# Attention layer of a two-layer encoder: key norms in a projection bank, key rounding ordered behind the exponential

## Chip, cores and metric

One core of a Trainium2 chip runs one program. The metric is the device time of one execution in microseconds (us), median over runs.

## What is computed

Two sequences of 512 tokens, each with 16 meta tokens in front (T = 528), go through two layers. Layer one is a gated DeltaNet and is not touched. Layer two is an attention over 16 heads whose queries and keys are normalised by their root mean square. Cut to what matters here:

```python
kv = (ckv @ w_ukv).reshape(B, L, 16, 128 + 128)
k = concat([kv[..., :128], broadcast(k_pe)])      # 192 wide
k = k * rsqrt(mean(k * k) + eps) * gain           # per token and head
s = einsum(q, k) * scale
o = softmax(s) @ v
y = (o * silu(z)) @ w_out
```

## The kernel before, in words

Every matmul operand is split into a rounded high half and a remainder (names ending in H and L, or wh and wl for weights), and three matmuls replace one (`mm3`, lines 74 to 76). ScalarE (ACT) rounds, VectorE (DVE) or GpSimd (POOL) subtracts (the helper at line 87). Weights come in on SyncE's queue (SP) as `wraw` (L210), ACT rounds them to `wh` (L213), POOL makes `wl`.

Layer two works in 16 units of two heads, eight per sequence. `run` writes the order of the program by hand: for step n = 0 to 7 of a unit (two heads times four query blocks) it issues a piece of the next unit's head, then the scores of the next step, then the output of this step. The head's pieces are: n=0 `pair_k` (key projection, four halves, each in a bank tagged `pj`, and the norms of the keys), n=1 `pair_qrope`, n=2 `pair_z` of this unit's second head, n=3 `pair_q` of the first head, n=4 `pair_v`, n=5 `pair_q` of the second head and `pair_knorm` twice, n=6 `pair_z` of the next unit's first head. A scheduler then orders each engine's instructions; within one engine they run in that order, and a waiting instruction holds up those behind it.

PSUM has eight banks: `pj` two, `S` (scores) two of two banks each, `tr` one, `x` one. In `x` lie, in program order per unit, the sums of squares of the keys (L966, n=0), the output products of steps 1 and 3 (L1099 is their last matmul), the sums of squares of the queries (L995, n=5) and the output products of steps 5 and 7.

The way of the key norms: `pair_k` copies the projected keys to `kr` (L959, ACT; one buffer), squares them (L961, L962, ACT), adds them up in `sqH` (L963, POOL), sums over the partitions with 12 small matmuls (L966, PE), adds the shared term (L967, DVE), takes the power -1/2 (L91, POOL, `rk`), writes to memory (L971) and reads it back broadcast to all partitions as `rs` (L973), both on SP. `pair_knorm` multiplies: `kr` by `rs` (L1030, DVE), rounded to `kH` (L378, ACT) with remainder `kL` (L87, DVE); and the shared rotary part by `rs` into `acc` (L1033, POOL), rounded to `kst` (L1035, ACT), remainder by DVE. `pair_knorm` is traced inside `issue_after` blocks, which put each of its instructions on an engine behind a given instruction of that same engine: on POOL behind the last `wl`, on DVE behind the last row maximum `mx` (L1064). On ACT it has no such order.

One step of attention: scores on PE (L74 to L76, L1060, L1061), `mx` (L1064, L1065, DVE), exponential to `P` (L1068, ACT), its scaling (L1069, L1071, DVE), transposes (L1083 for the meta tokens, into the used score bank, L1085 into `tr`), rounding and remainders (`pst` L1088, L1089; `hnH` L1091), output product in `x`, and L1100 (DVE), which reads `x`. The gate of `pair_z` is a tanh on ACT (L1046) and a product on DVE (L1047), which frees the `pj` bank.

Of the kernel before, what the change touches and what calls it, by code (L numbers as in the profile page):

```python
# [11 lines left out]
AF = mybir.ActivationFunctionType  # L12
# [11 lines left out]
class Trunk:  # L24
    def __init__(self, ctx, tc, ins, outs):
        self.tc, self.nc, self.ins, self.outs = tc, tc.nc, ins, outs
        self.ctx = ctx
        self.cn = ctx.enter_context(tc.tile_pool(name="cn", bufs=1))
        self.dr = ctx.enter_context(tc.tile_pool(name="dr", space=DRAM, bufs=1))
        self.sa = ctx.enter_context(tc.tile_pool(name="sa", bufs=1, reuse_waits="tile"))  # L30
        self.n = 0
        self.inner = None
        self.last_mx = None
        self.next_pool(self.BUFS1, self.PBUFS1)

    def next_pool(self, bufs, pbufs):
# [909 lines left out]
    def pair_k(self, u):  # L946
        nc = self.nc
        V, A, G, PE = nc.vector, nc.scalar, nc.gpsimd, nc.tensor
        UKV, c, hs = self.ins["mla_w_ukv"][0], u["c"], u["hs"]
        ckv = c["ckv"]  # L950
        kr = u["kr"] = self.t("kr", [128, 2, T])
        rk = self.t("rk", [88, 2, 6])
        kk = self.t("sqH", [128, T])
        sq = self.t("raw", [128, T])
        for j, h in enumerate(hs):
            w = self.weights([(0, UKV[:, 256 * h:256 * h + 128])], 2, hk=2)
            for c0 in KC:
                ps = self.project(w, ckv, 2, c0, 264)
                A.copy(kr[:, j, c0:c0 + 264], ps)  # L959
            o, nn = self.SIDES[j]  # L960
            A.activation(kk[o], kr[nn, j], AF.Square)  # L961
            A.activation(sq[o], kr[o, j], AF.Square)  # L962
            G.tensor_tensor(kk[o], kk[o], sq[o], op=ALU.add)  # L963
        ps = self.p("x", [88, 6, 2])
        for i in range(6):
            PE.matmul(ps[:, i], kk[:, 88 * i:88 * i + 88], self.two, start=True, stop=True)  # L966
        V.scalar_tensor_tensor(rk, ps.rearrange("p i j -> p j i"), 1.0 / 192, c["kss"].unsqueeze(1).to_broadcast([88, 2, 6]), op0=ALU.mult, op1=ALU.add)  # L967
        rf = rk.rearrange("p j i -> p (j i)")
        self.rsqrt(rf, rf)
        rkd = self.d("rkd", [2, T])  # L970
        nc.sync.dma_start(rkd.rearrange("j (i p) -> p j i", p=88), rk)  # L971
        rs = u["rs"] = self.t("rs2", [128, 2, T])
        nc.sync.dma_start(rs, rkd.rearrange("j t -> (j t)").unsqueeze(0).to_broadcast([128, 2 * T]).rearrange("p (j t) -> p j t", j=2))  # L973
# [75 lines left out]
    def pair_scores(self, u, j, qt):  # L1049
        nc = self.nc  # L1050
        V, A, G, PE = nc.vector, nc.scalar, nc.gpsimd, nc.tensor
        (qH, qL), (kH, kL) = u["q"][j], u["k"][j]
        SQ, RL, kst, qs = u["SQ"], u["RL"], u["kst"][j], u["qs"]
        cs = slice(128 * qt, 128 * qt + 128)
        S = self.p("S", [128, 2, 512])
        for ci, c0 in enumerate(KC):
            kc = slice(c0, c0 + 264)
            so = S[:, ci, 0:264]
            self.mm3(so, (qH[:, cs], qL[:, cs]), (kH[:, kc], kL[:, kc]), last=False)
            PE.matmul(so, SQ[j][:, cs], kst[:, kc], start=False, stop=False)  # L1060
            PE.matmul(so, RL[j][:, cs], kst[:, kc], start=False, stop=True)  # L1061
        Sv = S[:, :, 0:264]
        mx = self.t("mx", [128, 1])
        self.last_mx = V.tensor_reduce(mx, Sv, axis=AX.XY, op=ALU.max, negate=True)  # L1064
        V.tensor_scalar(mx, mx, qs[j][:, qt:qt + 1], None, op0=ALU.mult)  # L1065
        P = self.t("P", [128, 2, 264])
        sm = self.t("sm", [128, 1])
        A.activation(P, Sv, AF.Exp, bias=mx, scale=qs[j][:, qt:qt + 1], accum_out=sm)  # L1068
        V.reciprocal(sm, sm)  # L1069
        P = P.rearrange("p a b -> p (a b)")  # L1070
        V.tensor_scalar(P, P, sm, None, op0=ALU.mult)  # L1071
        u["SP"] = S, P
# [31 lines left out]
    def run(self, rc, rs):  # L1104
# [76 lines left out]
        def head(u):  # L1181
            self.pair_k(u)
            yield
            self.pair_qrope(u)
            yield
            if u["hp"]:
                yield
            self.pair_q(u, 0)
            yield
            if u["hp"]:  # L1190
                self.pair_v(u)
                yield
            self.pair_q(u, 1)
            with ExitStack() as behind:
                for x in [self.last_wl] + ([self.last_mx] if self.last_mx is not None else []):
                    behind.enter_context(self.tc.issue_after(x.ins))
                self.pair_knorm(u, 0)
                self.pair_knorm(u, 1)
            yield
            self.pair_z(u, 0)  # L1200
            yield
            if u["hp"] == 0:
                self.pair_v(u)
                yield
# [13 lines left out]

        ends = [self.out_proj(y2[s], I["mla_w_out"][0], h1[s], hq[s], NM, 512, [tC, tA], finish(s)) for s in range(2)]
        fill = chain(self.l2_prep(0, h1[0], rsd[0], ctx[0]), head(units[0]))  # L1220
        S = self.p("S", [128, 2, 512])
        pss[1] += [S[:, c, 0:264] for c in range(2)]
# [10 lines left out]
        for i, u in enumerate(units):  # L1233
            edge = i % 8 == 7
            if not edge:
                fill = head(units[i + 1])
            else:
                fill = chain(self.l2_prep(1, h1[1], rsd[1], ctx[1]), head(units[8])) if i == 7 else ends[0]
            zat = 0 if i == 15 else 2
            for n in range(8):  # L1240
                if n == zat and i != 7:
                    self.pair_z(u, 1)
                for _ in range((2, 1, 2, 2, 2, 2, 2, 2)[n] if i == 7 else int(n > 0 or not edge)):
                    next(fill, None)
                if i == 6 and n == 7:
                    self.pair_z(units[7], 1)
                S, P = u["SP"]
                if n < 7:
                    self.pair_scores(u, (n + 1) // 4, (n + 1) % 4)
                elif i == 7:  # L1250
                    drain(fill)
                    self.pair_scores(units[8], 0, 0)
                elif i < 15:
                    self.pair_scores(units[i + 1], 0, 0)
                self.pair_out(u, n // 4, n % 4, S, P)
# [48 lines left out]
```

## Time and profile before

| | us |
|---|---|
| median of three runs (lowest, highest) | 2698.04 (2696.45, 2699.07) |
| the profiled execution | 2700.19 |
| its span, first to last instruction | 2698.5 |
| PE busy | 2500.3 (93%) |
| DVE busy | 1755.9 (65%) |
| ACT busy | 1452.6 (54%) |
| POOL busy | 1270.0 (47%) |
| mean granted clock of PE | 0.957 |

Layer two's attention runs from about 1560 to 2480 us of the span. [...] Busy time of PE is modelled and counts a matmul at half clock in full length, so idle time and half clock have to be read separately.

### The profile page before, as it was taken

Reading aid. Unit: us, or ns where it says so; the run is one execution under the profiler, and the core shown is the slowest. Engines: PE = TensorE matmul, PEld = TensorE weight load, DVE = VectorE, ACT = ScalarE, POOL = GpSimd, SP = SyncE. Lnnn points to the kernel's source line nnn. Section 1 sums busy time; section 2 is a strip of 40 time slices with the busy share of each in tenths; the row PEclk is TensorE's granted clock in tenths of the full one; section 3 lists DMA queues with packets and bytes.
Section 4 is the critical chain, followed back from the end, with each engine's and each line's share of the span. In section 5 each row is a group of like instructions: output and inputs, shape, how many; then the busy total and the mean of one; then the engine's idle time right before and its main releaser. Section 6 shows DMA issues by size and latency. Waiting matters only on the chain. (4 is left out here: it accounts for less than half of the span.)

```text
span 2698.5 us, 51896 instructions
## 1 busy us (share of the span) xinstructions
PE 2500.3 (93%) x19083; PEld 2237.2 (83%) x19083; DVE 1755.9 (65%) x3915; ACT 1452.6 (54%) x3522; POOL 1270.0 (47%) x1255
## 2 busy tenths in 40 slices
PE   8899999999999999899999999998998989999999
PEld 7888888878888888788989888887887878887787
DVE  6888887777897777886554356555665656566421
ACT  5445555556555555645545466555556555655432
POOL 5544554435445444533445555444436454544243
PEclk9999999989999999989999899999999999999999
DMA  3222222221222243225475423232322322225475
GB/s 101 67 51 59 56 62 57 70 61 48 62 63 59 53 125 83 78 70 152 121 229 160 125 73 80 67 66 73 91 79 76 79 67 71 66 66 152 136 231 148
DMA packets 448511, 245.14 MB, mean 91 GB/s; under 512 B 131132, under 2 KB 408878, under 8 KB 448256
## 3 DMA queue, kind: packets, MB, share of 16 engines
q1 hardware_dynamic: 448256, 241.82, 33.6%
q8 instruction: 150, 2.46, 0.4%
q14 instruction: 105, 0.86, 0.1%
HBM read 190.72 MB, written 42.08 MB: 86 GB/s over the span
## 5 line engine op out<-in xcount | busy, mean ns | idle before, releaser
L87 POOL TENSOR_TENSOR wl<-wraw,wh 128x512 fp32r<-128x512 f32 (+2 forms) x512 | 661.5, 1294 | 805.4 <-ACT wh L213 744.4
L74 PE MATMUL pj<-hnH,wh 128*128 128x264 f32 (+4 forms) x2080 | 634.1, 306 | 20.0 <-DVE zs L624 10.6
L76 PE MATMUL pj<-hnH,wl 128*128 128x264 f32 (+3 forms) x2080 | 633.6, 306 | 0.5 <-POOL wl L87 0.5
L75 PE MATMUL pj<-hnL,wh 128*128 128x264 f32 (+3 forms) x2080 | 628.9, 303 | 4.5 <-DVE hnL L774 4.5
L213 ACT CAST wh<-wraw 128x512 fp32r<-128x512 f32 (+2 forms) x512 | 306.9, 602 | 312.7 <-PE pj L75 203.2
L74 PEld LDWEIGHTS pj<-hnH,wh 128*128 128x128 f32 (+1 forms) x2080 | 402.5, 194 | 37.6 <-DVE zs L624 12.5
L75 PEld LDWEIGHTS pj<-hnL,wh 128*128 128x128 f32 (+1 forms) x2080 | 402.7, 194 | 18.6 <-DVE hnL L774 5.1
L76 PEld LDWEIGHTS pj<-hnH,wl 128*128 128x128 f32 (+1 forms) x2080 | 401.9, 193 | 15.5 <-issue 3.7
L74 PE MATMUL pj<-h2H,wh 128*128 128x512 f32 (+1 forms) x544 | 207.0, 383 | 5.0 <-ACT h2H L769 3.0
L76 PE MATMUL pj<-h2H,wl 128*128 128x512 f32 (+1 forms) x544 | 207.3, 382 | 0.0
L75 PE MATMUL pj<-h2L,wh 128*128 128x512 f32 (+1 forms) x544 | 206.2, 380 | 0.7 <-DVE h2L L87 0.7
L1064 DVE TENSOR_REDUCE mx<-S 128x1 f32<-128x528 f32 x128 | 89.7, 702 | 77.1 <-PE S L1061 76.7
L74 PEld LDWEIGHTS pj<-h2H,wh 128*128 128x128 f32 x544 | 103.1, 191 | 24.7 <-ACT h2H L769 3.5
L364 DVE SCALAR_TENSOR_TENSOR acc<-raw,vec,acc 128x528 f32<-128x528 f32 x128 | 117.5, 921 | 4.4 <-ACT acc L362 3.3
L75 PEld LDWEIGHTS pj<-h2L,wh 128*128 128x128 f32 x544 | 103.2, 190 | 18.9 <-DVE h2L L87 2.1
L76 PEld LDWEIGHTS pj<-h2H,wl 128*128 128x128 f32 x544 | 103.4, 190 | 17.9 <-POOL wl L87 0.2
L1068 ACT ACTIVATE P<-S,mx,qs 128x528 f32<-128x528 f32 x128 | 101.2, 790 | 31.0 <-DVE mx L1065 29.9
L364 DVE SCALAR_TENSOR_TENSOR kq<-raw,vec,kq 128x528 f32<-128x528 f32 x128 | 110.6, 864 | 9.4 <-ACT kq L362 8.4
L783 DVE TENSOR_TENSOR raw<-raw,pj 128x512 f32<-128x512 f32 (+1 forms) x54 | 31.2, 580 | 125.1 <-PE pj L76 117.8
L722 POOL TENSOR_TENSOR oa<-oa,ot 128x256 f32<-128x256 f32 (+1 forms) x80 | 68.2, 853 | 81.1 <-DVE ot L720 80.9
L87 DVE TENSOR_TENSOR hnH<-tr,hnH 128x512 fp32r<-128x512 f32 x128 | 87.8, 686 | 27.6 <-ACT hnH L1091 26.0
L494 DVE TENSOR_TENSOR Yt<-Bl,Y 66x15 f32<-66x15 f32 (+7 forms) x240 | 85.5, 356 | 23.4 <-POOL Bl L486 18.9
(483 smaller groups left out, 6848.2 us busy)
## 6 DMA issues: line engine op xcount, KB each, us to landing
wraw<-in_gdn_w_in_dram SPq DMA_DIRECT2D x192, 256.0 KB
wraw<-in_mla_w_in_dram SPq DMA_DIRECT2D x88, 256.0 KB
wraw<-in_gdn_w_out_dram SPq DMA_DIRECT2D x64, 256.0 KB
wraw<-in_mla_w_out_dram SPq DMA_DIRECT2D x64, 256.0 KB
acc<-y SPq DMA_DIRECT2D x32, 264.0 KB
rs<-rkd SPq DMA_DIRECT2D x16, 528.0 KB
y<-y SPq DMA_DIRECT2D x64, 128.0 KB
wraw<-in_mla_w_ukv_dram SPq DMA_DIRECT2D x64, 128.0 KB
```

The source lines that it names most:

```text
L74: mm(out, ah, bh, start=first, stop=False)
L75: mm(out, ah, bl, start=False, stop=False)
L76: mm(out, al, bh, start=False, stop=last)
L87: return eng.tensor_tensor(out, a, hi, op=ALU.subtract)
L213: nc.scalar.copy(wh, raw)
L364: nc.vector.scalar_tensor_tensor(acc, raw[:, j:j + T], self.convw(j, u), acc, op0=ALU.mult, op1=ALU.add)
L494: V.tensor_tensor(tv, Bl[:, r + 1:16, r:r + 1].to_broadcast([66, m, c]), Y[:, r:r + 1, 0:c].to_broadcast([66, m, c]), op=ALU.mult)
L722: G.tensor_tensor(oa[:n, i], oa[:n, i], t, op=ALU.add)
L783: nc.vector.tensor_tensor(r[:, c0:c0 + chunk], r[:, c0:c0 + chunk], ps, op=ALU.add)
L1064: self.last_mx = V.tensor_reduce(mx, Sv, axis=AX.XY, op=ALU.max, negate=True)
L1068: A.activation(P, Sv, AF.Exp, bias=mx, scale=qs[j][:, qt:qt + 1], accum_out=sm)
```

## The change

The sums of squares of the keys get a bank tagged `pj` instead of `x`. The last exponential is remembered, and `pair_knorm`'s ACT instructions (both `kH` and both `kst`) are put behind it. At that point of the program the last maximum and the last exponential are those of step 5, the second query block of the unit's second head. (The program traces `pair_knorm` at n=5, when the scores of step 5 have been traced.) Nothing is computed differently.

```diff
-        self.last_mx = None
+        self.last_mx = self.last_P = None
...
             G.tensor_tensor(kk[o], kk[o], sq[o], op=ALU.add)
-        ps = self.p("x", [88, 6, 2])
+        ps = self.p("pj", [88, 6, 2])
         for i in range(6):
             PE.matmul(ps[:, i], kk[:, 88 * i:88 * i + 88], self.two, start=True, stop=True)
...
-        A.activation(P, Sv, AF.Exp, bias=mx, scale=qs[j][:, qt:qt + 1], accum_out=sm)
+        self.last_P = A.activation(P, Sv, AF.Exp, bias=mx, scale=qs[j][:, qt:qt + 1], accum_out=sm)
...
             with ExitStack() as behind:
-                for x in [self.last_wl] + ([self.last_mx] if self.last_mx is not None else []):
+                for x in [self.last_wl] + ([self.last_mx, self.last_P] if self.last_mx is not None else []):
                     behind.enter_context(self.tc.issue_after(x.ins))
                 self.pair_knorm(u, 0)
                 self.pair_knorm(u, 1)
```

## Rows read from the trace of the kernel before

**Rows 1.** Page, part 1: busy time, share of the span, instructions.
```profile
PE 2500.3 (93%) x19083; PEld 2237.2 (83%) x19083; DVE 1755.9 (65%) x3915; ACT 1452.6 (54%) x3522; POOL 1270.0 (47%) x1255
```

**Rows 2.** PE's waits, 1560 to 2480 us: total, times, longest.
```profile
PE pj L74 <- DVE zs L1047: 34.9, 8, 5.7
PE pj L74 <- DVE hnL L87: 16.5, 3, 7.4
...
PE pj L74 <- ACT kr L959: 8.5, 17, 1.0
```

**Rows 3.** One unit: stretch, length, busy PE, PEld, DVE, ACT, POOL, PEclk, DMA share, GB/s.
```profile
2204.74:2263.63 58.89, 51.96 (x332) 46.60 (x331) 34.83 (x73) 33.38 (x76) 26.48 (x20) 0.94 0.27 68
```

**Rows 4.** PE in order of time, parts of that unit: start, length, [idle before, releaser].
```profile
2204.74 1.03 PE L966 MATMUL x<-two,sqH 128*88 128x2 f32 x12
...
2218.84 0.40 PE L76 MATMUL pj<-h2H,wl 128*128 128x512 f32 x1
...
2220.16 0.36 PE L76 MATMUL pj<-ckvH,wl 128*128 128x264 f32 x1
2225.87 0.59 PE L74 MATMUL pj<-ckvH,wh 128*128 128x264 f32 x1 [5.35 <-DVE zs L1047]
...
2229.33 0.42 PE L1061 MATMUL S<-kst,RL 128*128 128x264 f32 x1
...
2235.76 0.39 PE L74 MATMUL pj<-ckvH,wh 128*128 128x264 f32 x1 [0.55 <-ACT kr L959]
...
2237.20 0.28 PE L76 MATMUL pj<-ckvH,wl 128*128 128x264 f32 x1
...
2238.41 0.50 PE L74 MATMUL pj<-cqH,wh 128*128 128x512 f32 x1 [0.38 <-ACT kr L959]
```

**Rows 5.** DVE in order of time, the same unit.
```profile
2225.12 0.69 DVE L1047 SCALAR_TENSOR_TENSOR zs<-zs,pj 128x512 f32<-128x512 f32 x1 [5.36 <-ACT zs L1046]
...
2232.92 0.21 DVE L1065 TENSOR_SCALAR mx<-mx,qs 128x1 f32<-128x1 f32 x1
```

**Rows 6.** ACT in order of time, the same unit.
```profile
2223.45 0.63 ACT L1035 CAST kst<-acc 128x528 fp32r<-128x528 f32 x1 [7.13 <-POOL acc L1033]
...
2224.50 0.59 ACT L1046 ACTIVATE zs<-pj 128x512 f32<-128x512 f32 x1
...
2233.84 0.79 ACT L1068 ACTIVATE P<-S,mx,qs 128x528 f32<-128x528 f32 x1
...
2235.33 0.66 ACT L959 COPY kr<-pj 128x264 f32<-128x264 f32 x2 [0.61 <-DVE kL L87]
...
2238.78 0.38 ACT L959 COPY kr<-pj 128x264 f32<-128x264 f32 x1
```

**Rows 7.** POOL in order of time, the same unit.
```profile
2207.65 2.27 POOL L91 TENSOR_TENSOR rk<-rk,mhalf 88x12 f32<-88x12 f32 x1
...
2222.11 2.55 POOL L1033 TENSOR_TENSOR acc<-kpr,rs 128x528 f32<-128x528 f32 x2 [6.79 <-DMA rs<-rkd]
...
2241.64 1.34 POOL L963 TENSOR_TENSOR sqH<-sqH,raw 64x528 f32<-64x528 f32 x1 [1.15 <-PE S L1083]
```

**Rows 8.** SP's queue in order of time, the same unit.
```profile
2209.94 0.32 SPq L971 DMA_DIRECT2D rkd<-rk  x1
...
2217.06 0.34 SPq L973 DMA_DIRECT2D rs<-rkd  x1
```

**Rows 9.** Waits of POOL and ACT, 1560 to 2480 us: total, times, longest.
```profile
POOL acc L1033 <- DMA rs<-rkd: 91.2, 14, 9.7
...
ACT kst L1035 <- POOL acc L1033: 92.1, 14, 7.5
```

**Rows 10.** Stretches after an idle time of PE, columns as in rows 3.
```profile
2226.00:2228.00 2.00, 2.00 (x9) 2.00 (x10) 1.38 (x4) 1.46 (x4) 0.00 (x0) 0.50 0.35 100
...
2174.00:2180.00 6.00, 5.04 (x21) 4.69 (x21) 2.91 (x8) 5.03 (x13) 4.28 (x3) 0.50 0.00 0
```

**Rows 11.** PE in order of time, another unit.
```profile
2172.47 0.39 PE L74 MATMUL S<-kH,qH 128*128 128x264 f32 x1 [2.17 <-DVE pst L87]
```

## The prediction

> **What bounds the kernel now.** I read the page first: PE is busy 93% of the span, all others far less [rows 1], so only time that PE idles or runs slowly is to be had. PE's own list of waits for the attention of layer two then says where it idles: most of it is projections (`pj`) that wait for DVE's gate product `zs` or a remainder `hnL`, in spells of up to 7.4 us [rows 2]. Third, one unit by its stretch: 58.89 us, of which PE is idle 58.89 - 51.96 = 6.93, at a mean clock of 0.94 [rows 3]. Six other stretches from one L966 to the next look like it, in length within 1.3 us and with the same clock.
>
> Last, the order of time around the long gap, read backwards. PE waits 5.35 us with the key projection, for a bank that the gate product frees [rows 4]; DVE's gate product waits 5.36 us for ACT's tanh [rows 5]; the tanh's input was finished at 2218.84 + 0.40 = 2219.24, but it stands on ACT behind the rounding of `kst`, which waits 7.13 us for POOL [rows 6]; and POOL waits 6.79 us for `rs` to land [rows 7]. The memory trip is late since it starts late: SP issues the write at 2209.94, and the read only at 2217.06, when the write has landed [rows 8]. Nor is that a single case: POOL waited for `rs` 14 times, 91.2 us, and ACT 14 times for POOL, 92.1 us [rows 9]. The idle spell has a second price: behind it PE runs at 0.50 of its clock [rows 10]. Over the unit 0.06 x 58.89 = 3.5 us go that way. At full clock and without idle time a unit would take 58.89 - 6.93 - 3.5 = 48.5 us.
>
> **Part one: sums of squares in a projection bank.** The 12 small matmuls stay, 1.03 us per unit [rows 4]. Before, they came right after an output product had left `x`, since `x` is handed on in program order. The squares of the next unit are complete at 2241.64 + 1.34 = 2242.98 [rows 7], and its small matmuls run at 2263.63, where the stretch of rows 3 ends [rows 3]: some 20 us spent waiting for the bank alone. In `pj` they stand behind the key projection and ahead of the rotary query projection, so I put them at about 2243. Moved with them are L967 on DVE, POOL's 2.27 us for `rk` [rows 7] and both DMAs on SP. `rs` then lands about 20 us earlier, well before POOL's wait of 6.79 us begins. On SP the loads of weights now queue behind the read's wait (2209.94 to 2217.06, 7 us [rows 8]) at an earlier place; POOL's weight halves queue behind `rk` there. Both were queued behind the same two steps before, once per unit, and PE was not held by them [rows 2]; I take nothing, with 0 to 2.3 us per unit (POOL's 2.27) as bounds.
>
> The cost is in PE's banks. With 13 groups per unit instead of 12 in two banks, (c) the rotary projection gets the bank of the last key half, whose copy ends at 2238.78 + 0.38 = 2239.16 [rows 6], where PE had started it at 2238.41 [rows 4]: 0.75 more beside the 0.38 already waited, so 1.1 idle. (d) The gate projection after it gets the bank of the small matmuls, free at about 2242.98 + 1.03 + 0.5 for DVE = 2244.5. PE would come there at about 2242.1, with a score group and the small matmuls (about 2.2 us) at hand: 0 to 2.4 us idle, I take 0.5.
>
> **Part two: rounding behind the exponential.** `kst` no longer holds up ACT while `rs` is under way: the wait of 7.13 us [rows 6] goes even if `rs` comes no sooner. (a) The tanh and gate product then follow the projection's end at 2219.24 by 0.59 + 0.69 and some handing over [rows 5, 6], about 2220.9, and PE has the first key half done at 2220.52 [rows 4]: 0.4 idle instead of 5.35.
>
> What is late next is (b) the buffer `kr`. The next key half may not be copied out before both `kL` are made, and those follow step 5's maximum. From the end of step 5's scores, 2229.33 + 0.42 = 2229.75, to PE's next key half at 2235.76 are 6.0 us [rows 4]. Now the exponential stands ahead: it can start after L1065, at 2232.92 + 0.21 [rows 5], takes 0.79 and 0.2 for its sum, and two `kH` and one `kst` at about 0.6 follow before the copy, which moves by about 1.3 us: a chain of 7.3. PE's own work in between was 6.0 - 0.55 = 5.5 us [rows 4], partly at half clock, so about 4.5 at full clock. Idle 2.8, where 0.55 showed before: the slow clock had covered the chain. Queued behind the rounding on ACT are the `kr` copies and the next exponential; the first scores of the next unit, which need the keys, come behind those of two more steps on PE, and are not held.
>
> **The sum.** Idle per unit: 0.4 (a) + 2.8 (b) + 1.1 (c) + 0.5 (d) + 0.5 for other short waits = 5.3 us. Unit: 48.5 + 5.3 = 53.8, so 5.1 us gained if the clock stays up, of which 3.5 are the clock. I count seven regular units in full and the other seven of the 14 stalls [rows 9], whose gaps lie elsewhere, by half: 10.5 x 5.1 = 54 us. From the profiled execution's 2700.2 that is 2646, from the median, 2.2 lower, 2644. Best bound: (b) filled by reordered work and all 14 in full, 14 x 7.5 = 105 us, 2593.
>
> **Rivals.** *The clock falls all the same.* Several short waits would take the place of one long one. For it: at 2174 to 2180 us the clock was 0.50 [rows 10] although no single wait just before exceeded 2.17 us [rows 11]. Against: single waits near 0.5 us left it at 1.00 in the regular units. The gain is then 5.1 - 3.5 = 1.6 per unit, 10.5 x 1.6 = 17 us: 2681; with 1.6 us more idle it is nothing: 2698. [...]
>
> *The small matmuls hold PE: slower.* PE's order is fixed beforehand. If they stand ahead of the rotary projection, PE waits from the last key half's end, 2237.20 + 0.28 = 2237.48 [rows 4], to 2242.98 [rows 7], 5.5 us, less 0.6 for transposes: 4.9 instead of the 1.6 in (c) and (d). With the clock down again that is 3.3 + 3.5 - 5.1 = 1.7 us lost per unit, 14 x 1.7 = 24 us: 2722. It decides from 1.6 us more idle than I count, given the low clock. For it: the squares pass through ACT and POOL, which are later than planned in this trace already (7.13 us). Against: the rotary projection is ready before them and needs no such wait.
>
> *The norms come no sooner* (SP or POOL orders `rk` late). Then part two alone acts, POOL's wait stays, but little of PE's hangs on it: about 2650, inside the forecast.
>
> **How the numbers follow.** Forecast, with its variant of late norms: 0.66, 2644; own range 2596 to 2668. Clock rival 0.20: 0.13 of it faster by over 0.2% (5.4 us, about what a measurement of this kernel can tell from no change), 0.06 within, 0.01 slower. Slower rival 0.14: 0.13 slower, 0.01 within. Together 0.79, 0.07, 0.14. The range goes from near the best bound, 2596, through most of the clock rival, 2693; what lies outside is the slower rival and little else.
>
> **What would show it.** Right: ACT's wait of `kst` for POOL and POOL's for `rs` nearly gone, L966 some 20 us earlier in the unit, PE's wait on `zs` under 1 us, units near 54 us, clock near 1.00 in most; PE's waits on `kr` larger than before. Wrong: the clock at 0.94 in units without a long gap (first rival), or a new PE wait of 3 us or more on `sqH` at L966 or on `rk` ahead of the gate projection (second).

## The result, and the profile after

The changed kernel takes 2709.18 us (median of 20 executions) where the kernel before, run beside it, takes 2693.94 (20): ratio 1.0056, 95% interval 1.0040 to 1.0071. One of its 20, at 3330.96 us with a granted clock of 0.65, is left out of the ratio. It is slower by half a per cent. The forecast was 2644, the range 2596 to 2693: the time lies above both and moved the other way.

The page of the changed kernel, part 1 (span 2704.5 us, granted clock 0.959; before 2698.5 and 0.957), answers to [rows 1]:

```profile
PE 2492.2 (92%) x19083; PEld 2232.3 (83%) x19083; DVE 1790.8 (66%) x3915; ACT 1447.1 (54%) x3522; POOL 1282.5 (47%) x1255
```

PE's waits after, 1560 to 2480 us, as in [rows 2] (total, times, longest):

```profile
PE S L1083 <- DVE P L1071: 55.3, 21, 5.4
PE S L74 <- DVE pst L87: 14.8, 14, 1.2
PE pj L74 <- DVE qL L987: 11.0, 15, 2.5
...
PE pj L966 <- POOL sqH L963: 4.0, 14, 0.5
...
PE pj L74 <- DVE zs L1047: 0.7, 1, 0.7
...
PE pj L74 <- ACT kr L959: 0.3, 1, 0.3
```

What the prediction wanted gone is gone: the wait on `zs` fell from 34.9 to 0.7 us, that on `kr` from 8.5 to 0.3. In its place stands a wait that the kernel before hardly had: the transposes of L1083 wait 21 times, 55.3 us, for the scaled exponential of L1071. Two units after and a stretch within the first, columns as in [rows 3]:

```profile
2197.75:2256.59 58.84, 52.62 (x331) 47.18 (x331) 37.55 (x73) 32.91 (x76) 27.59 (x20) 0.91 0.27 68
2256.59:2315.07 58.48, 50.60 (x331) 45.38 (x331) 37.39 (x73) 32.93 (x76) 27.57 (x20) 0.97 0.26 69
...
2222.00:2229.00 7.00, 6.37 (x29) 5.80 (x28) 6.01 (x11) 4.24 (x12) 2.72 (x2) 0.50 0.19 50
```

A unit is as long as before (58.89), its idle time as large (58.84 - 52.62 = 6.2 against 6.9), and again a stretch at half clock (0.50 from 2222 to 2229 us) follows the gap. The next rows are the chain behind the gap, in order of time by engine (SP, ACT, POOL, DVE, PE), after:

```profile
2201.62 0.32 SPq L971 DMA_DIRECT2D rkd<-rk  x1
2208.49 0.35 SPq L973 DMA_DIRECT2D rs<-rkd  x1
2208.89 0.42 SPq L1102 DMA_DIRECT2D y<-zs  x1
2209.36 2.50 SPq L830 DMA_DIRECT2D acc<-acc  x4
...
2204.12 0.70 ACT L930 ACTIVATE acc<-pj,vec 128x512 f32<-128x512 f32 x1
2204.71 0.60 ACT L932 ACTIVATE sqr<-pj 128x512 f32<-128x512 f32 x1
...
2219.28 1.26 ACT L941 CAST SQ<-acc 64x512 fp32r<-64x512 f32 x2 [6.59 <-DVE acc L937]
...
2196.37 1.32 POOL L963 TENSOR_TENSOR sqH<-sqH,raw 64x528 f32<-64x528 f32 x1 [1.07 <-ACT raw L962]
...
2214.96 1.30 POOL L935 TENSOR_TENSOR acc<-acc,rc 128x512 f32<-128x512 f32 x1 [6.49 <-DMA acc<-acc]
...
2217.51 1.74 DVE L937 TENSOR_TENSOR acc<-acc 128x512 f32<-128x512 f32 x1 [6.01 <-POOL acc L936]
...
2219.85 0.85 DVE L1071 TENSOR_SCALAR P<-P,sm 128x528 f32<-128x528 f32 x1
...
2220.84 0.37 PE L1083 MATMUL S<-ident,P 128*16 128x128 f32 x1 [4.21 <-DVE P L1071]
```

Read it backwards. PE waits 4.21 us for L1071, which stands on DVE behind L937, the sum of the rotary query. L937 waits for POOL, and POOL waits 6.49 us for the four transfers of L830, which swap the halves of the rotary query (POOL's L935 writes over the tile that they read, so it too has to wait for all four). Their source was ready at 2204.12 + 0.70 = 2204.82. SP issues them at 2209.36: it had issued the write of `rk` at 2201.62 and then stood until 2208.49, when that write had landed and the read of `rs` could go out. Nothing in the swaps needs the norms; they only stand behind them on SP. The waits over the attention say that it is every unit (POOL, ACT, then SP; `rs` itself makes POOL wait once now, 14 times in [rows 9]):

```profile
POOL acc L935 <- DMA acc<-acc: 82.1, 13, 7.7
...
POOL acc L1033 <- DMA rs<-rkd: 5.4, 1, 5.4
...
ACT SQ L941 <- DVE acc L937: 87.6, 15, 7.8
...
SPq L971 <- POOL rk L91: 86.4, 15, 6.2
SPq L973 <- DMA rkd<-rk: 85.8, 15, 6.6
```

### The profile page after: what moved, and what is told of

The parts are those of the page before. It is cut to its first block, busy times and chain, and to the rows that moved or that the text cites. A ratio compares the mean times of both kernels' runs of the same rounds, so it can differ in the third digit from the quotient of the medians.

```text
span 2704.5 us, 51852 instructions
## 1 busy us (share of the span) xinstructions
PE 2492.2 (92%) x19083; PEld 2232.3 (83%) x19083; DVE 1790.8 (66%) x3915; ACT 1447.1 (54%) x3522; POOL 1282.5 (47%) x1255
## 5 line engine op out<-in xcount | busy, mean ns | idle before, releaser
L1068 ACT ACTIVATE P<-S,mx,qs 128x528 f32<-128x528 f32 x128 | 101.4, 792 | 57.1 <-DVE mx L1065 55.8
L1091 ACT CAST hnH<-tr 128x512 fp32r<-128x512 f32 x128 | 75.0, 586 | 95.9 <-PE tr L1085 94.0
```

What stands on the lines that cost most here:

```text
L1068: self.last_P = A.activation(P, Sv, AF.Exp, bias=mx, scale=qs[j][:, qt:qt + 1], accum_out=sm)
L1091: A.copy(PTH[:, :, hc], pt)
```

## The experiments

Every kernel was timed beside the kernel before on its own chip (whose median was 2686 to 2705 us), so ratios are compared. Theory Q, and R, into which it grew: the gain of part two is real, and part one gives it back because the write of `rk` and the read of `rs` move ahead of the swaps on SP. Against it stood theories by which the bank tagged `pj` costs by itself. The table measures the swaps in each profile: median over the 15 units of the time from the end of the rotary square (L932, shortly after the swaps' source is ready) to SP's first swap, to POOL's product (L935), which has to wait for all four, and to ACT's rounding (L941), worked out from the rows of ACT, SP and POOL in order of time. The fourth column is the median of the second minus the first, unit by unit.

| kernel | first swap | POOL's product | ACT's rounding | issue to product | ratio [95%] |
|---|---|---|---|---|---|
| before | -0.5 | 3.7 | 7.7 | 4.1 | 1 |
| after | 3.3 | 9.3 | 13.6 | 5.7 | 1.0056 [1.0040, 1.0071] |
| e1_edge_only | -0.5 | 3.6 | 8.0 | 4.1 | 0.9845 [0.9826, 0.9865] |
| e2_bank_only | 3.6 | 9.8 | 14.1 | 5.9 | 1.0090 [1.0073, 1.0107] |
| e3_swaps_first | -0.5 | 3.6 | 7.3 | 4.0 | 1.0077 [1.0060, 1.0094] |
| e4_read_behind_swaps | -0.5 | 6.1 | 10.5 | 6.6 | 0.9842 [0.9798, 0.9887] |
| e5_edge_and_pool_order | -0.5 | 3.6 | 8.0 | 4.1 | 0.9666 [0.9643, 0.9688] |
| e6_both_orders | -0.5 | 6.1 | 10.7 | 6.6 | 0.9872 [0.9847, 0.9897] |
| e7_no_round_trip | -0.5 | 6.6 | 11.0 | 7.1 | 0.9876 [0.9847, 0.9905] |
| e8_swaps_first_pool | -0.5 | 3.6 | 7.3 | 4.1 | 0.9742 [0.9704, 0.9779] |
| e9_pool_order_only | -0.5 | 3.6 | 8.0 | 4.1 | 0.9788 [0.9760, 0.9816] |
| e10_write_on_pool_queue | -0.5 | 7.3 | 11.7 | 7.8 | 0.9915 [0.9887, 0.9943] |
| e11_small_write_first | 0.4 | 9.0 | 12.9 | 8.6 | 0.9979 [0.9951, 1.0007] |
| e12_row_write_first | 0.4 | 4.7 | 8.9 | 4.3 | 0.9739 [0.9705, 0.9773] |

### The two parts alone

**e1** takes the kernel before and part two (the edge on ACT) alone.

```diff
-                for x in [self.last_wl] + ([self.last_mx] if self.last_mx is not None else []):
+                for x in [self.last_wl] + ([self.last_mx, self.last_P] if self.last_mx is not None else []):
```

> Part two alone (rounding behind the exponential; the sums of squares stay in bank x). Theory Q, the queue: the changed kernel is held by the rotary swaps, whose four DMAs stand on SP behind the read of rs. Here that read stays late in the unit and the swaps stand ahead of it as before, so ACT waits neither for kst nor for SQ: 30 to 55 us faster than before, 2640 to 2665. Rival C, the chain: behind any removed wait the chain maximum, exponential, key rounding, kr holds PE and the clock falls again: within 10 us of before.

**e2** takes the kernel before and part one alone:

```diff
-        ps = self.p("x", [88, 6, 2])
+        ps = self.p("pj", [88, 6, 2])
```

> Part one alone (sums of squares in a projection bank; no order behind the exponential). Theory Q: rs comes early, so the wait of ACT for kst goes, but the swaps stand behind rs on SP and ACT waits 6 to 8 us per unit for SQ instead: near the changed kernel, 2695 to 2715. Rival E, that the order behind the exponential is what costs: 30 us or more faster than before.

e1 gains 1.55%, 2686.33 to 2644.76; e2 loses 0.9%, at 2710.84. Both times lie in the ranges of theory Q, but ACT's wait for `SQ`, which it wanted gone in e1, is 43.9 us there (15.1 before). In the changed kernel part one takes 1.0056 - 0.9845 = 2.1 points from what part two gives alone. The swaps are late in e2 as in the changed kernel and on time in e1 (table). In e1 `rs` still lands late, and what it holds up next is seen in two rows of its waits (POOL, DVE): POOL waits for it, and DVE for the query squares (L989), which are queued behind that product on POOL:

```profile
POOL acc L1033 <- DMA rs<-rkd: 80.0, 12, 8.1
...
DVE sqr L990 <- POOL sqr L989: 55.8, 15, 7.6
```

### The round trip behind the swaps

**e3** is the changed kernel with the write and the read both behind the unit's swaps on SP (line numbers shift by a few):

```diff
-        self.swap(sw, qg, 512)
+        with self.tc.issue_after(self.swap(sw, qg, 512).ins):
+            self.key_norms(u)
...
+        u["rk"] = rk
+
+    def key_norms(self, u):
+        nc, rk = self.nc, u["rk"]
         rkd = self.d("rkd", [2, T])
```

> The changed kernel with the write and read of rk and rs issued on SP behind the rotary swaps of the same unit, nothing else changed. Theory Q: POOL's wait for the swaps falls from about 6 us to under 1.5 us per unit, ACT's wait for SQ goes, and the time falls to 2640 to 2665. Rival C: another wait takes the place, 2690 or more.

A miss: 1.0077, though the swaps are on time. The time is lost elsewhere, seen in rows of SP and POOL in order of time and in one of PE's waits, e3:

```profile
2207.00 2.46 SPq L830 DMA_DIRECT2D acc<-acc  x4
2209.56 0.48 SPq L977 DMA_DIRECT2D rkd<-rk  x1
...
2216.94 0.34 SPq L979 DMA_DIRECT2D rs<-rkd  x1
...
2223.57 2.56 POOL L1039 TENSOR_TENSOR acc<-kpr,rs 128x528 f32<-128x528 f32 x2 [7.85 <-DMA rs<-rkd]
...
2227.30 1.26 POOL L995 TENSOR_TENSOR sqr<-sqr,raw 64x512 f32<-64x512 f32 x1
...
PE pj L74 <- DVE hnL L87: 57.7, 14, 6.0
```

From the issue of the write to POOL's start it takes 2223.57 - 2209.56 = 14.0 us. POOL stands for 7.85 of them, the query squares (L995) queue behind, DVE behind these, and PE waits 57.7 us for DVE's `hnL`. So place on SP alone does not decide: in the changed kernel the swaps stand behind the trip's wait on SP (6.9 us in the unit shown), in e3 the query squares stand behind its wait on POOL (7.85 us).

**e4** moves the read alone behind the swaps; the write stays where the change put it.

```diff
         nc.sync.dma_start(rkd.rearrange("j (i p) -> p j i", p=88), rk)
+        u["rkd"] = rkd
+
+    def key_norms(self, u):
+        nc, rkd = self.nc, u["rkd"]
         rs = u["rs"] = self.t("rs2", [128, 2, T])
```

> The changed kernel with only the read of rs issued on SP behind the rotary swaps; the write of rk stays ahead of them, so its landing passes while the swaps go out. Theory R, the round trips: the changed kernel loses its gain since engines that work in order meet a tile whose DMA has not landed (first the swaps behind rs, with the swaps moved ahead rs itself at POOL). Here both should have landed when they are met: POOL's waits for the swaps and for rs under 3 us per unit together, 2630 to 2660. Rival B, the bank: the 13th group in the two projection banks costs by itself what the edge gains, whatever the DMAs do: 2690 or more.

0.9842: 2.1 points come back. The time, 2661.08, is just above theory R's range and far under rival B's. SP no longer stands for the landing ahead of the swaps, and their issue is on time. But they take 6.6 us from issue to POOL's product, where they took 4.1, and POOL still waits 44.9 us for them.

**e7** is the changed kernel with `rs` read from a table written once at the start. It leaves out the use of the key norms; `rk` is still made and written.

```diff
-        nc.sync.dma_start(rs, rkd.rearrange("j t -> (j t)")...
+        nc.sync.dma_start(rs, self.rk0.rearrange("j t -> (j t)")...
```

> The changed kernel with rs read from a table written once at the start of layer two, so that the read waits for nothing; the sums of squares, rk and its write stay. It leaves out the use of the key norms. Theory R: SP no longer stands on the read, the swaps go out when ready, and the time falls by 40 to 90 us, 2620 to 2670. Rival B: it stays at 2690 or more.

0.9876, no better than e4, at 2673.16 again just above the range: with the wait for the landing gone altogether, the swaps are still 2.9 us later at POOL than before (6.6 against 3.7), issued on time. (The read does wait for something: SP stands 59.2 us at it, 12 times, for DVE, but the swaps do not stand behind that.)

### The order on POOL

**e5** is e1 with one edge more: POOL's product with `rs` goes behind POOL's addition of the query squares.

```diff
-        G.tensor_tensor(sqr[o], sqr[o], sq[o], op=ALU.add)
+        self.last_sqr = G.tensor_tensor(sqr[o], sqr[o], sq[o], op=ALU.add)
...
-                for x in [self.last_wl] + ([self.last_mx, self.last_P] if self.last_mx is not None else []):
+                for x in [self.last_wl, self.last_sqr] + ([self.last_mx, self.last_P] if self.last_mx is not None else []):
```

> Part two alone, and POOL's part of the key norms (acc) also put behind the addition of the query squares of the same unit, which so far waited behind it on POOL. Theory R: DVE's wait for those squares (55.8 us in 15 waits with part two alone) falls below 15 us and the time falls by another 15 to 40 us, 2605 to 2630. Rival C, the chain: PE is held by the chain of maximum, exponential and key rounding by now, the removed wait is replaced: 2640 to 2655, as with part two alone.

0.9666, the fastest of all, 2617.77 against 2705.11. POOL's wait for `rs` is 31.0 us, 8 times (80.0, 12 times in e1), and DVE's wait for the query squares is 5.2 us (55.8). Theory R holds. **e6** is e4 with that edge, **e8** is e3 with it, **e9** the kernel before with it and without the edge on ACT.

> The read of rs behind the swaps and POOL's part behind the query squares, both in the changed kernel. Theory R: at or below the better of the two single ones, 2600 to 2640. Rival B: 2690 or more.

> e3 with one thing more: POOL's product acc (L1039) is also put behind POOL's addition of the query squares, as in e5. Theory R (the round trip on SP decides, the bank itself costs nothing): rs still lands late, but what waits on POOL for it no longer has the query squares behind it, so DVE's wait for sqr (69.1 us in e3) and PE's wait for hnL at L74 (57.7) fall under 20 us each, and the ratio is near that of e5: 0.965 to 0.98. Rival B (the bank tagged pj costs by itself, since projections and small matmuls now share two banks): PE shows waits at projections that e5 has not, and the ratio stays at 0.985 to 1.005.

> The kernel before with e5's order on POOL alone: no edge on ACT, bank x. If the edge on ACT is what brings the gain (R: kst stands at the head of ACT and waits for POOL, whatever POOL does before it), ACT's wait of kst for acc stays at 80 us or more (92.1 before) and the ratio is 0.99 to 1.01. If instead the order on POOL alone lets the work through (rival: e5's gain is POOL's), the ratio is 0.985 or less.

e6 is a miss: no gain over e4. It could have none, since `rs` lands early there and POOL does not wait for it; its swaps are as late as in e4. e8 goes from e3's 1.0077 to 0.9742, in the range of theory R, with DVE's wait for the query squares down to 3.6 us and PE's for `hnL` no longer in its list; this shows that what was queued on POOL behind the late `rs` was e3's loss. e9 is a miss as well: 0.9788, where theory R had no gain, since `kst` at the head of ACT was to be what costs. Its row of ACT's waits answers to [rows 9]:

```profile
ACT kst L1035 <- POOL acc L1033: 55.1, 13, 8.6
```

Behind the query squares POOL comes to its product later, and `kst` after it; ACT stands for 55.1 us instead of 92.1. The late `rs` did harm in two places, at POOL and at ACT. Each order alone wins 1.5 to 2.1%, both together 3.3%.

That the bank costs by itself is limited by e8 against e5: 0.8 points, some 20 us (0.2 to 1.4 points between the ends of the two intervals), with the swaps on time in both. Two rows of PE's waits in e8, where e5 has neither among its largest, come to as much; that these are the whole difference is not shown:

```profile
PE pj L74 <- DVE qL L993: 16.3, 14, 2.3
...
PE pj L968 <- POOL sqH L965: 3.7, 14, 0.5
```

### Why the swaps land late

**e10** is e6 with the write of `rk` issued by POOL's own queue.

```diff
-        nc.sync.dma_start(rkd.rearrange("j (i p) -> p j i", p=88), rk)
+        nc.gpsimd.dma_start(rkd.rearrange("j (i p) -> p j i", p=88), rk)
```

> e6 with the write of rk to memory issued by POOL's queue, right behind rk, instead of by SP's; the read stays on SP behind the swaps. Theory R: SP no longer stands for rk (87.9 us in e6), the swaps go out when their sources are there, POOL's wait of acc for the swaps falls from about 45 us to under 25, and the ratio goes from 0.987 to 0.965 to 0.98. Rival B (the bank costs by itself): the swaps' wait falls as well, but the ratio stays at 0.985 or above. Rival W (a write issued by POOL takes much longer to land, or holds POOL): POOL's wait of acc for rs grows beyond 60 us and the ratio stays above 0.985.

0.9915, a miss for each of the three: SP no longer stands for `rk` (88.1 us in e6), the swaps are issued on time as in e6, and they land later still: 7.8 us from issue to product, with POOL's wait for them up from 42.9 us to 59.4 and none listed for `rs`. (The 87.9 and about 45 us in the expectation are e4's values.) So the write is not in the way on SP's queue only (7.8 us here, 7.1 in e6). It is 1056 values of 4 bytes, scattered. **e11** is e5, whose swaps take 4.1 us, with such a write, which nobody reads, put ahead of the swaps; **e12** writes the same values in 88 pieces of 48 bytes.

```diff
-        self.swap(sw, qg, 512)
+        xd = self.d("xd", [2, T])
+        x = nc.sync.dma_start(xd.rearrange("j (i p) -> p (j i)", p=88), sqr[0:88, 0:12])
+        with self.tc.issue_after(x.ins):
+            self.swap(sw, qg, 512)
```

From e11 to e12:

```diff
-        xd = self.d("xd", [2, T])
-        x = nc.sync.dma_start(xd.rearrange("j (i p) -> p (j i)", p=88), sqr[0:88, 0:12])
+        xd = self.d("xd", [88, 12])
+        x = nc.sync.dma_start(xd, sqr[0:88, 0:12])
```

> e5, with one more write to memory on SP right ahead of the four swaps of every unit: 1056 values of 4 bytes out of sqr, scattered as the write of rk is; nobody reads them. Theory C (the many small pieces of such a write delay the transfers that are issued right behind it): from the first swap's issue to POOL's acc (L938 here) it takes 6 to 8 us, as in e4, e6 and e10, where e5 has 4.1; the ratio goes from 0.967 to 0.975 to 0.99. Rival (only the place in SP's order counts): 4 to 4.5 us from issue to POOL's acc, swaps about 1 us later for the added issue, ratio 0.965 to 0.972.

> e11 with the same 1056 values written in 88 pieces of 48 bytes. Theory C: the swaps land as in e5, 4 to 4.8 us from the first issue to POOL's acc, and the ratio is 0.965 to 0.973. If any write ahead of the swaps delays them, whatever its pieces, it stays at 6 to 8 us and the ratio at that of e11.

One unit of e11: SP's two issues, POOL's product, and the packets of the 10 us from 2187:

```profile
2187.44 0.32 SPq L935 DMA_DIRECT2D xd<-sqr  x1
2187.80 2.52 SPq L830 DMA_DIRECT2D acc<-acc  x4
...
2196.70 1.29 POOL L938 TENSOR_TENSOR acc<-acc,rc 128x512 f32<-128x512 f32 x1 [4.42 <-DMA acc<-acc]
...
DMA packets 2054, 0.67 MB, mean 67 GB/s; under 512 B 1147, under 2 KB 1926, under 8 KB 2054
```

The same of e12, packets of the 10 us from 2203.5:

```profile
2203.82 0.32 SPq L935 DMA_DIRECT2D xd<-sqr  x1
2204.18 2.45 SPq L830 DMA_DIRECT2D acc<-acc  x4
...
2208.84 1.48 POOL L938 TENSOR_TENSOR acc<-acc,rc 128x512 f32<-128x512 f32 x1
...
DMA packets 1348, 0.80 MB, mean 80 GB/s; under 512 B 195, under 2 KB 1219, under 8 KB 1347
```

Issued 0.36 us behind the write in both, the swaps reach POOL after 8.9 us in e11 and 4.7 in e12; the medians are 8.6 and 4.3. The packets under 512 B differ by 952, about what 1056 pieces against 88 make. Theory C has the direction of both right: e11 goes beyond its two ranges, e12 is inside the first and just above the second. The time is 0.9979 against 0.9739: 2.4 points, 65 us (60 by the medians), or 4.0 to 4.3 us for each of 15 units, where the product is 8.9 - 4.7 = 4.2 us later. Between these two a microsecond by which the swaps land later is a microsecond of the unit. It is not so everywhere: e4's swaps reach POOL 2.5 us later than e1's at the same ratio, and e1 has the waits for `rs` shown above, which e4 has not. (The scheduler's order of the matmuls differs a little between the two kernels, as between most kernels here; that part of the difference isn't separated.)

What is late is not the bytes, and the delay goes by the write. The next rows are packets of e11 from 2187 to 2189 (the pieces) and from 2189 to 2191.5 (the 207 - 79 = 128 of 2 KB or more, 0.26 MB, are the four swaps), and of the changed kernel from 2203.5 to 2208.49, while SP stands for the landing of the write:

```profile
DMA packets 1052, 0.00 MB, mean 2 GB/s; under 512 B 1052, under 2 KB 1052, under 8 KB 1052
...
DMA packets 207, 0.26 MB, mean 105 GB/s; under 512 B 79, under 2 KB 79, under 8 KB 207
...
DMA packets 0, 0.00 MB, mean 0 GB/s; under 512 B 0, under 2 KB 0, under 8 KB 0
```

In e11 the swaps' packets have started by 2191.5, and POOL is released at 2196.70, 5.2 us later; in the changed kernel SP stands for 5.0 us in which no packet starts. Counted from the issue of the write, in the same rows as the table, the median to POOL's product is 9.6 us in e4, 9.7 in e6, 9.5 in e7 and 8.9 in e10 and e11, wherever in these microseconds the swaps are issued; in e12 it is 4.6. Why a write in such pieces takes so long to land is not shown; e12 changes the number and the size of the pieces together.

## Why the prediction was wrong

**The step that failed** is in part one: "I take nothing, with 0 to 2.3 us per unit" for SP's and POOL's queues, since "both were queued behind the same two steps before, once per unit, and PE was not held by them". It costed only what had stood behind the steps at the old place. It named the loads of weights, and not the swaps, which at the new place stand on SP behind the read and one store. Measured there: swaps issued 3.3 + 0.5 = 3.8 us later, and 5.7 - 4.1 = 1.6 us slower from issue to product, behind the read and the store (the write had landed by then; what each of the two adds is not separated); POOL's product 9.3 - 3.7 = 5.6 us later, ACT's rounding 5.9. The bound of 2.3 was POOL's `rk` alone; SP's 7 us between write and read stood in the same paragraph. Of the forecast's 5.1 us per unit that was all: a unit of 58.84 instead of 53.8.

**Reading of before: right.** The chain from `zs` back to `rs` was the bound, and each cut of it pays (e1, e9, e5). It said that the trip was late because it started late; e5, where it starts late still and nothing critical queues behind it, is the fastest.

**Part one, the bank: right in place, sizes a little high.** L966 runs as early as said: at 2197.75, where POOL has the squares at 2196.37 + 1.32 = 2197.69; some 20 us of waiting for the bank are gone, and PE's waits at it are 0.5 us at most. Terms (c) and (d), 1.1 + 0.5 us per unit or 22 us in 14, did not come where they were named: the wait on `kr` of (c) is not there, and what there is are waits on `qL` (11.0 against 2.5), nearly all at the value projection, and at L966 (4.0): 12.5 us.

**Part two: (a) right, (b) did not come.** PE's wait on `zs` went. The 2.8 us per unit expected on `kr` are 0.3 us in the whole attention, and in e1 none is among PE's waits. That working moved the copy by 1.3 us but kept PE's own work ahead of it as it was. In the unit shown the scheduler has PE take up the keys' projection only at 2242.89, behind the next query and gate projections, when ACT has rounded both `kH` (by 2238.31).

**The rivals.** *The small matmuls hold PE* had the right sign and the wrong place: they do stand ahead of the rotary projection, but score matmuls fill the time before, and the wait at L966 is 4.0 us in all. *The norms come no sooner* gave about 2650 for part two alone; e1's 0.9845 of the median of 2698.0 is 2656. That is near by luck: it held that little of PE's hangs on POOL's wait, and e5, which moves the query squares out from behind it, wins 1.8 points more. *The clock falls all the same*: in the changed kernel it falls with one gap of 4.21 us (1.00 from 2206 to 2218 us, 0.50 from 2222 to 2229), so it follows the new wait and explains nothing by itself; over the attention its mean is 0.94 where it was 0.95, and none of the 3.5 us per unit came back. A milder form of this rival is in e5, seen in PE's waits in order of time and in the stretch behind them:

```profile
2179.08 0.27 PE L1083 MATMUL S<-ident,P 128*16 128x128 f32 x1 [0.50 <-DVE P L1071]
...
2180.88 0.39 PE L74 MATMUL x<-hnH,hnL 128*128 128x256 f32 x1 [1.09 <-ACT hnH L1091]
...
2182.13 0.39 PE L74 MATMUL S<-kH,qH 128*128 128x264 f32 x1 [0.87 <-DVE pst L87]
...
2183.60:2186.80 3.20, 3.20 (x17) 3.20 (x16) 2.23 (x3) 1.99 (x4) 1.32 (x1) 0.50 0.02 5
```

Three idles of at most 1.09 us, and then 3.2 us at half clock (0.50; 1.00 in the 5.6 us before). In this one place the trace agrees with the rival; that the idles make the clock fall is not shown. Over the attention e5's mean clock is 0.98.

## What to carry to other kernels

When a step moves earlier, list for every queue that it passes what will stand behind it at the new place, and cost each wait of the step against the first of these that somebody needs; that the queue was harmless at the old place says nothing. A transfer that waits for a landing belongs behind independent transfers that are due (0.9842 in e4, 1.0056 in the changed kernel), and the work that waits for it belongs at the end of its engine's queue: e5 let the norms land late and only moved what stood behind them (0.9666, e1 0.9845). Cost a write in many 4-byte pieces by the transfers issued behind it as well: here the four swaps took 8.6 us to POOL's product behind 1056 such pieces (e11), 4.3 behind 88 pieces of 48 bytes (e12), and 7.8 where POOL's queue issued the small pieces (e10).

## What the runs showed of the hardware that was not expected

In the changed kernel a write of 4.1 KB in 4-byte pieces kept SP from its dependent read for 2208.49 - 2201.62 = 6.9 us, and four transfers of 64 KB issued right behind such a write took 8.6 us to POOL's product, instead of 4.3 behind the same values in 88 pieces of 48 bytes (e11, e12). In the unit of e11 shown the swaps' packets had started by 2191.5 and their consumer was released at 2196.70, 5.2 us later, with the small write ahead of them. In e10, where the write went out on another queue, the consumer started as late behind the write as in e11 (8.9 us, the median in each). What holds the release back is not shown.

Another issuing queue did not avoid it: with the write on POOL's queue the swaps on SP's took 7.8 us (e10; 7.1 in e6). SP's 88.1 us of standing for `rk` in e6 were gone, and the swaps reached POOL no earlier (7.3 us after the rotary square in e10, 6.1 in e6).
